# Strassen products summed in the matmul banks and read in between, in the feed-forward layers and the gated unit

## The chip, the cores and the metric

The kernel runs on one core of one Trainium2 chip. The metric is the device time of one execution in microseconds (us); the time of the kernel before is the median of three runs. Engines are named as in the profile: PE (TensorE, with PEld for its weight loads), DVE (VectorE), ACT (ScalarE), POOL (GpSimd), SP (whose queue issues most loads).

## The reference, cut to what matters

A two-layer backbone over 1024 tokens of width 1024, all in fp32. Layer 0 mixes by long convolutions and differential attention, layer 1 by a gated unit over chunks of 128 tokens; each layer ends with a feed-forward net with a short convolution. The change touches what follows the attention of layer 0.

```
x = x + g1 * mix_x                                   # mix: (... ) @ w_out
h = modulate(rmsnorm(x, norm_ffn_g[i]), sh2, sc2)
a = dwconv3(h @ w_up, conv_w, conv_b)                # 1024 -> 2 x 2816, three taps over time
g, u = jnp.split(a, 2, axis=-1)
x = x + g2 * ((silu(g) * u) @ w_down)                # 2816 -> 1024
...
u, v = jnp.split(gelu(h @ w_in + b_in), 2, axis=-1)  # gated unit: 1024 -> 2 x 1024
s = einsum('gts,bnsgc->bntgc', w_s, layernorm(v)) + b_s
mix_x = (u * s) @ w_out
```

## The kernel before

Activations lie transposed, features on the 128 partitions and the 1024 tokens along a row. A product W^T h is made by one step of Strassen's scheme in Winograd's form: W and h are cut into halves both ways, and seven products M1 to M7 of half-sized blocks are taken, not eight. With U2 = M1 + M6 the blocks of the result are C11 = M1 + M2, C12 = U2 + M5 + M3, C21 = U2 + M7 + M4 and C22 = U2 + M7 + M5; C[i, l] holds the features of half i and the tokens of half l. Sums of blocks of W (S1 to S4, `wsums`) and of h (T1 to T4) are made on the way. Every fp32 operand is split into a rounded part and the rest (`hilo`): ACT casts it (L1152), then POOL or DVE subtracts (L128), and `mm3` adds three matmuls hi*hi, hi*lo and lo*hi in one bank. A bank holds 128 x 512 fp32; the pool `pb` has all eight. A "unit" `u` is a tile of 128 x 1024 fp32 in SBUF.

After the attention come: the output projection (`out_proj`), the up phase and down phase of the first feed-forward net, the up phase of the gated unit's half u, its half v, its output projection, and up and down phase of the second net.

An **up phase** (`up_steps`) goes pair by pair: two tiles of 128 output features, one from either half of W's columns, 22 pairs in a net and 4 in the gated unit. In a pair each product is 12 matmuls into one bank. M1 is copied by ACT to both halves of c1 (L1317); the six others are added by DVE where they belong (L1326), M5 in two places, so that DVE has seven additions of 128 x 512 that read a bank. `post` then hands c1 and c2 to generators: in a net four DVE operations of the short convolution (L124, u<-u,cols,u), a scaled copy and a SiLU on ACT (L1520, L1532), a product on DVE, and for each second pair four subtractions on POOL (`spill`), whose results are stored for the down phase. The first three pairs of a phase go product by product (`EARLY`), since M1 and M2 need only the first half of the normed tokens.

A **down phase** (`down_steps`) goes product by product: four banks, 11 tiles k of rows in a net (4 in the gated unit), 12 matmuls for each k, then `accum` adds the four banks to x with the gate (DVE, L124, x<-b,mods,x), M1, M6 and M7 to both halves of a row at once where they belong to two blocks. When both blocks of a half of the tokens are complete, its norm starts beside the next products (`norm`, through `Later`), which also makes the blocks B11 to T4 for the next phase. The gated unit's half v is of this kind, with `accum` of its own.

The program is written out in one order for all engines. `run` issues for each step the preparation of later steps (`prep`, mostly three steps ahead) before the step's own matmuls and evictions, and `Later` inserts the side work; each engine executes its instructions in the order in which they stand. Beside the first net's phases `mods1` computes the modulation vectors of layer 1 (DVE, L124, u<-wraw,siluc,u).

## Time and profile before

| | |
|---|---|
| three runs | 2901.98, 2897.4, 2897.93 us; median 2897.93 |
| profiled execution: span | 2897.8 us, within 0.2 us of the median |
| busy share of the span | PE 85%, PEld 67%, DVE 81%, POOL 56%, ACT 37% |
| first net: up phase, down phase | 1049 to 1557, 1557 to 1811 us |
| gated unit: u, v, output projection | 1811 to 1907, 1907 to 1996, 1996 to 2116 us |
| second net: up phase, down phase and end | 2116 to 2640, 2640 to 2898 us |

The profiled execution's own time is its span; nothing of note lies around it. The phases' borders are where PE begins the first product of each. PE's matmuls are pipelined, so a busy share under 100% in the table of stages is time in which PE had nothing that it could start. The names of tiles leave out their numbers, so `u` stands for every unit and `b` for every bank; what an instruction does is read from its line and its shapes.

### The profile page before, as it was taken

The page shows a single profiled execution, that of the slowest core. Times are in us where ns is not written, and L with a number is a line of the kernel's source. Part 1 is how long each engine was busy: PE and PEld are TensorE (multiplying, and loading weights), DVE is VectorE, ACT ScalarE, POOL GpSimd, SP SyncE. Part 2 cuts the span into 40 slices and gives each one's busy share as a digit, 9 for nine tenths or more (in the row PEclk, how much of TensorE's full clock was granted, in tenths as well). Part 3 has the DMA queues.
Part 4 walks back from the last instruction along what each step waited for, and adds up shares of the span by engine and source line. Part 5 has one row for each costly group of instructions (what it writes and reads, how often), then busy time and mean ns, then how long its engine had stood idle before and what let it go on. Part 6 is the DMA issues. An engine that isn't in the chain of part 4 may idle for free. (4 is left out here: it accounts for less than half of the span.)

```text
span 2897.8 us, 29893 instructions
## 1 busy us (share of the span) xinstructions
PE 2461.0 (85%) x10776; PEld 1949.6 (67%) x10776; DVE 2345.8 (81%) x2467; ACT 1075.4 (37%) x1561; POOL 1624.7 (56%) x986
## 2 busy tenths in 40 slices
PE   6899667777988679999998799899669999999897
PEld 2897556565766457777776687677547777776676
DVE  4666887866998889999998987859988888887944
ACT  2322011015764344433343344532254343344242
POOL 1323565545444755645556787535665655657785
PEclk9899878888999889999999999999889999999999
DMA  7243121256732412434347654153021323227322
GB/s 269 69 143 114 66 87 46 84 183 200 209 122 84 174 65 78 161 122 149 118 145 255 231 164 129 44 186 110 23 79 59 100 85 102 86 85 269 133 91 102
DMA packets 137572, 363.93 MB, mean 126 GB/s; under 512 B 12587, under 2 KB 25391, under 8 KB 135248
## 3 DMA queue, kind: packets, MB, share of 16 engines
q1 hardware_dynamic: 90768, 259.25, 27.8%
q10 hardware_dynamic: 46656, 102.78, 9.4%
q8 instruction: 85, 1.39, 0.2%
q14 instruction: 63, 0.52, 0.1%
HBM read 271.80 MB, written 90.18 MB: 125 GB/s over the span
## 5 line engine op out<-in xcount | busy, mean ns | idle before, releaser
L149 PE MATMUL b<-u,u 128*128 128x512 f32 x5780 | 1422.9, 404 | 199.0 <-POOL u L128 125.7
L149 PEld LDWEIGHTS b<-u,u 128*128 128x128 f32 x5780 | 1104.1, 195 | 504.7 <-POOL u L128 172.0
L128 POOL TENSOR_TENSOR u<-u,u 128x512 fp32r<-128x512 f32 (+2 forms) x641 | 1043.3, 1650 | 602.5 <-ACT u L1152 431.2
L128 DVE TENSOR_TENSOR u<-u,u 128x512 f32<-128x512 f32 (+2 forms) x569 | 641.1, 1156 | 169.9 <-ACT u L1152 91.4
L1152 ACT CAST u<-u 128x512 fp32r<-128x512 f32 x772 | 439.1, 616 | 584.9 <-DVE u L128 400.4
L124 DVE SCALAR_TENSOR_TENSOR u<-u,cols,u 128x1023 f32<-128x1023 f32 x176 | 301.2, 1714 | 11.2 <-ACT u L1520 9.9
L128 DVE TENSOR_TENSOR u<-u,b 128x512 f32<-128x512 f32 (+1 forms) x368 | 248.1, 690 | 19.1 <-PE b L149 12.8
L128 POOL TENSOR_TENSOR f<-f 128x256 f32<-128x256 f32 (+2 forms) x99 | 124.7, 1273 | 211.0 <-DVE f L128 183.1
L149 PE MATMUL b<-x,u 128*128 128x512 f32 x1008 | 242.9, 394 | 0.0
L149 PEld LDWEIGHTS b<-x,u 128*128 128x128 f32 x1008 | 188.6, 187 | 46.0
L128 DVE TENSOR_TENSOR f<-f 128x256 f32<-128x256 f32 (+3 forms) x178 | 178.6, 1052 | 1.1
L124 DVE SCALAR_TENSOR_TENSOR x<-b,mods,x 128x512 f32<-128x512 f32 (+1 forms) x140 | 125.0, 938 | 37.2 <-PE b L149 37.2
L149 PE MATMUL pj<-hh,whi 128*128 128x512 f32 x320 | 130.2, 407 | 24.7 <-DVE t L124 14.0
L1520 ACT ACTIVATE u<-u,cols 128x1024 f32<-128x1024 f32 x88 | 109.2, 1244 | 111.3 <-DVE u L128 97.3
L128 POOL TENSOR_TENSOR p<-p,p 128x1280 f32<-128x1280 f32 x27 | 79.5, 2945 | 97.0 <-ACT p L880 76.5
L149 PE MATMUL pj<-hh,wlo 128*128 128x512 f32 x320 | 127.6, 399 | 3.5 <-DVE wlo L128 1.9
L149 PE MATMUL pj<-hl,whi 128*128 128x512 f32 x320 | 128.9, 403 | 0.0
L1532 ACT ACTIVATE u<-u 128x1024 f32<-128x1024 f32 x44 | 46.7, 1061 | 211.3 <-DVE u L124 211.2
L128 POOL TENSOR_TENSOR wlo<-wraw,whi 128x1024 fp32r<-128x1024 f32 x24 | 63.7, 2655 | 76.9 <-ACT whi L143 73.8
L869 ACT ACTIVATE p<-s,nx 128x1280 f32<-128x1280 f32 x64 | 85.0, 1329 | 43.2 <-DVE nx L865 39.2
L149 PE MATMUL s<-f,f 128*128 128x512 f32 (+1 forms) x288 | 82.3, 416 | 17.5 <-ACT t L768 9.9
L865 DVE TENSOR_REDUCE nx<-s 128x1 f32<-128x1280 f32 x64 | 94.5, 1480 | 2.2 <-PE s L149 1.5
(215 smaller groups left out, 2984.7 us busy)
## 6 DMA issues: line engine op xcount, KB each, us to landing
u<-wup SPq DMA_DIRECT2D x88, 512.0 KB, 3.7
Td<-u ACTq DMA_DIRECT2D x66, 512.0 KB, 3.2
u<-Td SPq DMA_DIRECT2D x56, 512.0 KB, 4.4
wraw<-modw SPq DMA_DIRECT2D x48, 512.0 KB, 3.7
u<-wdown SPq DMA_DIRECT2D x40, 512.0 KB, 7.1
wraw<-modw0b SPq DMA_DIRECT2D x32, 512.0 KB, 4.7
xs<-x ACTq DMA_DIRECT2D x48, 256.0 KB, 2.2
x<-xs SPq DMA_DIRECT2D x24, 512.0 KB, 4.1
```

The lines of the kernel that those rows point to most:

```text
L124: eng.scalar_tensor_tensor(out=o, in0=a, scalar=sc, in1=b, op0=op0, op1=op1)
L128: eng.tensor_tensor(out=o, in0=a, in1=b, op=op)
L149: T.matmul(o, l, r, start=st, stop=sp)
L865: V.reduce_max(out=q.nx, in_=q.s, axis=AX.X, negate=True)
L869: A.activation(q.p[m], q.s, AF.Exp, bias=q.nx, accum_out=q.l[:, m : m + 1])
L1152: A.copy(out=t[:, H0], in_=x)
L1520: A.activation(a, c, AF.Identity, bias=col(f"fb{l}", f), scale=col(f"fw{l}1", f))
L1532: A.activation(g, g, AF.Silu)
```

## The change

In the up phases of both nets and of the gated unit, and in the down phases of both nets and the gated unit's half v, M6 is added by PE onto the bank of M1, M7 onto that of M6, and M3 onto that of M5 (`ONTO`). Between two products that share a bank the bank is read: after M1 (for C11), after M6 (U2, for C12), after M7 (U2 + M7, for C21 and C22), after M5 and after M3. So the second product's first matmul waits for that read. The order of the products changes (`UP_ORDER`, `DOWN_ORDER`) so that at least one other product lies between two on one bank. In an up phase ACT now copies M1, M5, M6 and M4 (128 x 512 each), and DVE adds M2, M3 and, in one instruction of 128 x 1024, M7; `post` follows M7. In a down phase `accum` adds seven results, M7 alone to both blocks (`WHERE2`). The half v adds its bias with the first result that reaches a half row, so the eight separate additions on POOL (`bias`) go. Since C12 and C22 are now complete before C21, the half of the tokens that is normed first is the second one before the gated unit (`LEAD`), with one product beside which it can run; the norm makes T1 first. The two output projections keep the old sums; the gated unit's takes M1 and M2 one after the other, without its special order for the last k. Matmuls, operand splits, `wsums`, convolution and loads stay as many as they were.

```diff
-N0 = ((1, 1), (6, 1), (1, 1), (1, 0))
+N0 = ((1, 1), (1, 6), (1, 1), (1, 0))
...
-DL, DP = (1, 5, 4, 4, 5), ((3, 3, 3, 3, 3, 5, 8),) + ((3,) * 7,) * 4
+DL, DP = (1, 5, 4, 4, 5), ((3, 3, 3, 3, 3, 5, 8),) + ((3,) * 7,) * 2 + ((2,) + (3,) * 6, (3,) * 7)
...
-    def mm(o, l, r, st, sp):
-        T.matmul(o, l, r, start=st, stop=sp)
-
-    def mm3(o, lh, ll, rh, rl, st=True, sp=True):
-        mm(o, lh, rh, st, False)
-        mm(o, lh, rl, False, False)
-        mm(o, ll, rh, False, sp)
+    def mm(o, l, r, st, sp, onto=False):
+
+        T.matmul(o, l, r, start=st and not onto, stop=sp, skip_group_check=onto)
+
+    def mm3(o, lh, ll, rh, rl, st=True, sp=True, onto=False):
+        mm(o, lh, rh, st, False, onto)
+        mm(o, lh, rl, False, False, onto)
+        mm(o, ll, rh, False, sp, onto)
...
-        R, c, x = box[0], HALF[l], list(x)
-        if l == 0:
+        R, c, x, s = box[0], HALF[l], list(x), sqs.s
+        lead = l == LEAD[s]
+        h0, h1 = HALF[LEAD[s]], HALF[1 - LEAD[s]]
+        if lead:
             Stream.T = {n: [None] * 4 for n in BLOCKS}
-        s = sqs.s
...
-            if l == 0:
-                block("B11", k, x[k][:, H0], E(E_11[s], k))
-                block("B21", k, x[k + 4][:, H0], E(E_21[s], k))
+            if lead:
+                block("B11", k, x[k][:, h0], E(E_11[s], k))
+                block("B21", k, x[k + 4][:, h0], E(E_21[s], k))
                 yield 1
-        if l == 0:
+        if lead:
             return
...
-            sub(e, t3[k], z[:, H1], y[:, H1])
-            sub(e, y[:, H1], y[:, H1], y[:, H0])               # T1
-            sub(e, y[:, H0], z[:, H1], y[:, H1])               # T2
-            block("T2", k, y[:, H0], E(E_2[s], k))
+            sub(e, t3[k], z[:, h1], y[:, h1])
+            sub(e, y[:, h1], y[:, h1], y[:, h0])
+            block("T1", k, y[:, h1], E(E_2[s], k))
+            sub(e, y[:, h0], z[:, h1], y[:, h1])
             yield k % 2
         for k in range(4):
-            block("T3", k, t3[k], E(E_3[s], k))
+            block("T2", k, x[k][:, h0], E(E_3[s], k))
             yield k % 2
         for k in range(4):
             y, z = x[k], x[k + 4]
-            sub(E(E_T[s], k), z[:, H0], z[:, H0], y[:, H0])     # T4
-            block("T4", k, z[:, H0], E(E_4[s], k))
+            sub(E(E_T[s], k), z[:, h0], z[:, h0], y[:, h0])
+            block("T4", k, z[:, h0], E(E_4[s], k))
             yield k % 2
-        for n, i in (("T1", 0), ("B22", 4)):
+        for n, i in (("B22", 0), ("T3", 4)):
             for k in range(4):
...
-                T[n][k] = hilo(x[i + k][:, H1], E(E_5[s], i + k), unit if i + k == 0 else xunit)
...
+                T[n][k] = hilo(x[4 + k][:, h1] if i == 0 else t3[k], E(E_5[s], i + k), xunit)
                 yield k % 2
...
+    ONTO = {"M6": "M1", "M7": "M6", "M3": "M5"}
+    UP_ORDER = ("M1", "M2", "M5", "M6", "M4", "M3", "M7")
+    DOWN_ORDER = ("M1", "M2", "M6", "M5", "M7", "M3", "M4")
+    WHERE2 = {"M1": [(0, 0)], "M2": [(0, 0)], "M6": [(0, 1)], "M5": [(1, 1)], "M7": [(1,)], "M3": [(0, 1)],
+              "M4": [(1, 0)]}
...
+    LEAD = (0, 1, 0, 0)
...
-            if m == "M6":
+            if m == "M5":
                 w1, w2 = st_.pop("w1"), st_.pop("w2")
                 s2 = wsums(w1[:, H0], w2[:, H0], w1[:, H1], w2[:, H1], E_U[s])
                 q.update({"M4": w2[:, H1], "M7": w1[:, H0], "M6": s2, "M5": w2[:, H0], "M3": w1[:, H1]})
...
-            ps = bank()
+            ps = st_[m, "ps"] = st_.pop((ONTO[m], "ps")) if m in ONTO else bank()
             wh, wl = st_.pop(m)
             for k in range(4):
                 kk = slice(k * P, (k + 1) * P)
-                mm3(ps, wh[:, kk], wl[:, kk], *Stream.T[BOF[m]][k], k == 0, k == 3)
+                mm3(ps, wh[:, kk], wl[:, kk], *Stream.T[BOF[m]][k], k == 0, k == 3, m in ONTO)
+            h0, h1 = HALF[LEAD[s]], HALF[1 - LEAD[s]]
             if m == "M1":
-                c1 = st_["c1"] = unit()
-                A.copy(out=c1.rearrange("p (a n) -> p a n", a=2), in_=ps[:, None, :].to_broadcast([P, 2, 512]))
-                return
-            c1 = st_["c1"]
-            if m == "M7":
+                st_["c1"] = unit()
+                A.copy(out=st_["c1"][:, h0], in_=ps)
+            elif m == "M2":
+                c = st_["c1"][:, h0]
+                add(V, c, c, ps)
+            elif m == "M5":
                 st_["c2"] = unit()
-            c2 = st_.get("c2")
-            for o, x in {"M2": [(c1, H0)], "M6": [(c1, H1)], "M4": [(c2, H0)], "M5": [(c2, H1), (c1, H1)],
-                         "M3": [(c1, H1)], "M7": [(c2, H1)]}[m]:
-                src = {"M7": c1, "M4": c2}.get(m, o)[:, x if m != "M4" else H1]
-                add(V, o[:, x], src, ps)
-            if m == "M3":
-                post(c1, c2)
-
-        return {m: Step(lambda m=m: use(m), lambda m=m: prep(m), (lambda m=m: load(m)) if m in ("M1", "M6") else None, UL[s],
-                        UP[s][ORDER.index(m)])
-                for m in ORDER}
+                A.copy(out=st_["c2"][:, h1], in_=ps)
+            elif m == "M6":
+                A.copy(out=st_["c1"][:, h1], in_=ps)
+            elif m == "M4":
+                A.copy(out=st_["c2"][:, h0], in_=ps)
+            elif m == "M3":
+                c = st_["c1"][:, h1]
+                add(V, c, c, ps)
+            else:
+                c = st_["c2"].rearrange("p (a n) -> p a n", a=2)
+                add(V, c, c, ps[:, None, :].to_broadcast([P, 2, 512]))
+                post(st_["c1"], st_["c2"])
...
+        return {m: Step(lambda m=m: use(m), lambda m=m: prep(m), (lambda m=m: load(m)) if m in ("M1", "M5") else None, UL[s],
+                        UP[s][UP_ORDER.index(m)])
+                for m in UP_ORDER}
...
-        out = [u[m] for m in ORDER for u in ss[: EARLY[s]]]
+        out = [u[m] for m in UP_ORDER for u in ss[: EARLY[s]]]
         for u in ss[EARLY[s] :]:
-            out += [u[m] for m in ORDER]
+            out += [u[m] for m in UP_ORDER]
...
+            onto = products is DOWN_ORDER and m in ONTO
             if k == 0:
-                banks[m] = [bank() for _ in range(4)]
+                banks[m] = banks.pop(ONTO[m]) if onto else [bank() for _ in range(4)]
             ps = banks[m]
...
         order = [(m, k) for m in products for k in range(nk)]
-        if products is ORDER and nk <= NK and not resident:        # the last k may come late
-            order = [(m, k) for m in ("M1", "M2") for k in range(nk - 1)] + [("M1", nk - 1), ("M2", nk - 1)] \
-                + order[2 * nk :]
         return [Step(lambda m=m, k=k: use(m, k), lambda m=m, k=k: prep(m, k), lambda m=m, k=k: load(m, k), DL[s],
-                     DP[s][ORDER.index(m)])
+                     DP[s][DOWN_ORDER.index(m)])
...
+        last = {"M2": (0, 0), "M4": (1, 0), "M5": (1, 1), "M3": (0, 1)} if where is WHERE else \
+            {"M2": (0, 0), "M7": (1, 1), "M3": (0, 1), "M4": (1, 0)}
...
+        accum = gated_sum(x, gate, where)
...
         def accum(m, j, p):
-            if m == "M1":
-                for t in (j, j + 4):
...
+            for i, l, first in {"M1": [(0, 0, 1)], "M2": [(0, 0, 0)], "M6": [(0, 1, 1)], "M5": [(1, 1, 1)],
+                                "M7": [(1, 0, 1), (1, 1, 0)], "M3": [(0, 1, 0)], "M4": [(1, 0, 0)]}[m]:
+                t = j + 4 * (l if LEAD[1] == 0 else 1 - l)
+                if v[t] is None:
                     v[t] = unit()
-                    A.copy(out=v[t].rearrange("p (a n) -> p a n", a=2), in_=p[:, None, :].to_broadcast([P, 2, 512]))
-                return
-            for i, l in {"M2": [(0, 0)], "M6": [(None, 1), (1, 0)], "M7": [(1, 0), (1, 1)], "M4": [(1, 0)],
-                         "M5": [(None, 1)], "M3": [(0, 1)]}[m]:
-                y = v[j + 4 * l]
-                if i is None:
-                    y, p_ = y.rearrange("p (a n) -> p a n", a=2), p[:, None, :].to_broadcast([P, 2, 512])
-                else:
-                    y, p_ = y[:, HALF[i]], p
-                add(V, y, y, p_)
-
-        def bias():
-            for t in range(NK):
-                add(E(E_B[0], t), v[t], v[t], k_["bv"])
-                yield 1
+                y = v[t][:, HALF[i]]
+                add(V, y, k_["bv"][:, HALF[i]] if first else y, p)
...
-                yield 1 - l
-            yield MIXWAIT
+                yield (1 - l) * (t % 2)
+            if l:
+                yield MIXWAIT
...
         def done(m):
-            if m == "M1":
-                Later.add(bias(), BW)
-            elif m == "M6":
+            if m == "M6":
                 Later.add(offsets())
                 Later.add(loads_u(), LW)
+            elif m == "M3":
+                Later.add(center(0))
             elif m == "M4":
-                Later.add(center(0))
-            elif m == "M3":
                 Later.add(center(1))
...
+        steps += down_steps(3, 4, ap["wso"], lambda m, k: None, bprep, acc, dn, (x, x_src), products=ORDER)
```

What stands on DVE in one pair of the second net's up phase, in the middle of the phase. Before (b_16089 is M6, b_16108 M7, b_16127 M4, b_16144 M5, b_16169 M3; the four rows of 128x512 without a b are `wsums`, the row of 128x1024 the gated product):

```order
L128 TENSOR_TENSOR u_16059<-u_16059,b_16089 128x512
L128 TENSOR_TENSOR u_16083<-u_16083,u_16040 128x1024
L128 TENSOR_TENSOR u_16121<-u_16059,b_16108 128x512
L128 TENSOR_TENSOR u_16014<-u_16014,u_16064 128x512
L128 TENSOR_TENSOR u_16161<-u_16064,u_16014 128x512
L128 TENSOR_TENSOR u_16064<-u_16064 128x512
L128 TENSOR_TENSOR u_16014<-u_16014,u_16161 128x512
L128 TENSOR_TENSOR u_16121<-u_16121,b_16127 128x512
L128 TENSOR_TENSOR u_16121<-u_16121,b_16144 128x512
L128 TENSOR_TENSOR u_16059<-u_16059,b_16144 128x512
L124 SCALAR_TENSOR_TENSOR u_16183<-u_16121,cols,u_16183 128x1023
L128 TENSOR_TENSOR u_16059<-u_16059,b_16169 128x512
```

After (b_15861 is M2, b_15881 M5 and then M3, b_15838 M1, M6 and M7 in turn):

```order
L128 TENSOR_TENSOR u_15851<-u_15851,b_15861 128x512
L124 SCALAR_TENSOR_TENSOR u_15875<-u_15706,cols,u_15875 128x1023 x2
L128 TENSOR_TENSOR u_15807<-u_15807,u_15856 128x512
L128 TENSOR_TENSOR u_15950<-u_15856,u_15807 128x512
L128 TENSOR_TENSOR u_15856<-u_15856 128x512
L128 TENSOR_TENSOR u_15875<-u_15875,u_15832 128x1024
L128 TENSOR_TENSOR u_15807<-u_15807,u_15950 128x512
L128 TENSOR_TENSOR u_15851<-u_15851,b_15881 128x512
L128 TENSOR_TENSOR u_15894<-u_15894,b_15838 128x1024
L124 SCALAR_TENSOR_TENSOR u_15971<-u_15894,cols,u_15971 128x1023 x2
```

Seven additions from banks have become three. The four sums of weights now stand behind the convolution of the pair before and ahead of the additions of M3 and M7, and the convolution's first operation on c2 (u_15894) stands right behind M7's addition, with ACT's scaled copy between the two.

What stands on ACT at the same places. Before (b_16046 is M1; L1317 copies it, L1520 is the convolution's scaled copy, L1532 the SiLU, L1152 a cast, DMA a store's issue):

```order
L1152 CAST u_16021<-u_16016 128x512
L1420 DMA Td_5969<-u_15991 128x2x512
L1520 ACTIVATE u_16040<-u_15970,cols 128x1024
L1152 CAST u_16043<-u_15867 128x512
L1317 COPY u_16059<-b_16046 128x1024
L1152 CAST u_16066<-u_15913 128x512
L1520 ACTIVATE u_16083<-u_15910,cols 128x1024
L1152 CAST u_16086<-u_15913 128x512
L1152 CAST u_16105<-u_15867 128x512
L1532 ACTIVATE u_16083<-u_16083 128x1024
L1413 DMA Td_5969<-u_16083 128x512
```

After (L1330 copies M1, L1336 M5, L1338 M6, L1340 M4; L1541 is the scaled copy, L1553 the SiLU, L1153 a cast):

```order
L1541 ACTIVATE u_15875<-u_15706,cols 128x1024
L1153 CAST u_15878<-u_15664 128x512
L1336 COPY u_15894<-b_15881 128x512
L1153 CAST u_15898<-u_15664 128x512
L1153 CAST u_15915<-u_15807 128x512
L1153 CAST u_15932<-u_15807 128x512
L1553 ACTIVATE u_15875<-u_15875 128x1024
L1338 COPY u_15851<-b_15838 128x512
L1153 CAST u_15955<-u_15856 128x512
L1430 DMA Td_5969<-u_15875 128x512
L1340 COPY u_15894<-b_15918 128x512
L1541 ACTIVATE u_15971<-u_15894,cols 128x1024
```

Three more copies from banks stand between casts and the pieces of the convolution: M6's stands behind the SiLU of the pair before, and two casts of the next pair have moved ahead of that SiLU and of the store.

## Rows read from the trace of the kernel before

**Rows 1.** Page, part 1: busy us, share of span, instructions by engine.

```profile
PE 2461.0 (85%) x10776; PEld 1949.6 (67%) x10776; DVE 2345.8 (81%) x2467; ACT 1075.4 (37%) x1561; POOL 1624.7 (56%) x986
```

**Rows 2.** Windows by stage: length, busy us (instructions) by engine, granted clock.

```profile
core 0: us, PE busy (x) PEld busy (x) DVE busy (x) ACT busy (x) POOL busy (x), PEclk, DMA share, GB/s
1049.00:1557.00 508.00, 462.15 (x1923) 365.47 (x1922) 482.11 (x471) 203.18 (x280) 270.94 (x160) 0.95 0.38 126
1557.00:1811.00 254.00, 226.61 (x982) 180.78 (x983) 210.93 (x193) 109.82 (x192) 193.90 (x120) 0.97 0.58 193
1907.00:1996.00 89.00, 83.48 (x364) 66.20 (x364) 70.45 (x92) 27.30 (x40) 46.21 (x28) 0.98 0.37 125
1996.00:2116.00 120.00, 89.41 (x390) 69.68 (x389) 106.52 (x122) 34.59 (x60) 75.32 (x55) 0.89 0.20 71
2116.00:2640.00 524.00, 468.61 (x1921) 364.66 (x1919) 445.91 (x435) 216.81 (x304) 313.03 (x196) 0.97 0.27 88
2640.00:2898.00 258.00, 226.31 (x949) 179.90 (x947) 160.89 (x159) 96.22 (x171) 192.23 (x132) 0.95 0.42 147
```

**Rows 3.** Timeline of PE, first down phase: start, us, operation, count.

```profile
1687.53 52.67 PE L149 MATMUL b<-u,u 128*128 128x512 f32 x231
```

**Rows 4.** Windows: steady pairs of both up phases, the first net's first.

```profile
1183.00:1542.00 359.00, 329.78 (x1406) 262.40 (x1405) 343.94 (x322) 134.42 (x180) 192.35 (x112) 0.97 0.41 135
2255.00:2626.00 371.00, 344.54 (x1435) 269.06 (x1433) 312.84 (x289) 139.28 (x187) 219.36 (x138) 0.99 0.28 91
```

**Rows 5.** DVE's groups, first steady stretch: count | busy, mean ns | idle before.

```profile
L128 DVE TENSOR_TENSOR u<-u,b 128x512 f32<-128x512 f32 x111 | 74.1, 678 | 1.4
```

**Rows 6.** DVE's waits, first steady stretch: us in total, times, longest.

```profile
DVE u L128 <- ACT u L1532: 5.2, 9, 0.6
```

**Rows 7.** DVE's waits, second steady stretch.

```profile
DVE u L128 <- POOL u L128: 37.8, 17, 3.3
DVE u L128 <- ACT u L1532: 10.0, 17, 0.6
DVE u L124 <- ACT u L1520: 6.9, 9, 0.8
```

**Rows 8.** Timeline of DVE in two pairs of the second net.

```profile
2424.53 0.68 DVE L128 TENSOR_TENSOR u<-u 128x512 f32<-128x512 f32 x1
...
2443.45 3.46 DVE L128 TENSOR_TENSOR u<-u,u 128x512 f32<-128x512 f32 x2 [2.48 <-POOL u L128]
2446.84 1.78 DVE L128 TENSOR_TENSOR u<-u 128x512 f32<-128x512 f32 x1
2450.23 2.06 DVE L128 TENSOR_TENSOR u<-u,b 128x512 f32<-128x512 f32 x3
```

**Rows 9.** Timeline of POOL in the second of these pairs.

```profile
2440.91 1.29 POOL L128 TENSOR_TENSOR u<-u 128x512 f32<-128x512 f32 x1
2442.15 7.60 POOL L128 TENSOR_TENSOR u<-u,u 128x512 fp32r<-128x512 f32 x5
```

**Rows 10.** DVE's groups after 1250 us that read banks, by form.

```profile
L124 DVE SCALAR_TENSOR_TENSOR x<-b,mods,x 128x1024 f32<-128x1024 f32 x48 | 59.5, 1273 | 4.5 <-PE b L149 4.5
L124 DVE SCALAR_TENSOR_TENSOR x<-b,mods,x 128x512 f32<-128x512 f32 x72 | 50.6, 740 | 32.7 <-PE b L149 32.7
...
L128 DVE TENSOR_TENSOR u<-u,b 128x1024 f32<-128x1024 f32 x8 | 9.5, 1213 | 0.0
```

**Rows 11.** POOL's groups, gated unit's u and v.

```profile
L128 POOL TENSOR_TENSOR u<-u,u 128x1024 f32<-128x1024 f32 x8 | 21.0, 2636 | 19.3 <-PE b L149 16.8 <-DVE u L128 2.5
```

**Rows 12.** Timeline of ACT in the pair of rows 9.

```profile
2447.00 0.62 ACT L1152 CAST u<-u 128x512 fp32r<-128x512 f32 x1 [5.84 <-DVE u L128]
...
2450.93 1.25 ACT L1520 ACTIVATE u<-u,cols 128x1024 f32<-128x1024 f32 x1 [3.31 <-DVE u L128]
...
2452.59 1.00 ACT L1317 COPY u<-b 128x1024 f32<-128x1024 f32 x1
```

**Rows 13.** Timeline of PE in the pair of rows 9.

```profile
2443.47 5.75 PE L149 MATMUL b<-u,u 128*128 128x512 f32 x24 [1.07 <-POOL u L128]
```

23 lines of the change are left out of this document (11 added, 12 removed).

## The prediction

> **What bounds the kernel now.** I read the page's busy shares first: no engine is full over the whole span, PE comes nearest with 85% [rows 1]. So the stages come next [rows 2]. The change touches those from 1049 us on: up and down phase of the first net (508 and 254 us), the gated unit, up and down phase of the second net (524 and 258 us). Undisturbed, PE needs 52.67/231 = 0.228 us for a matmul [rows 3]; a pair of an up phase is 84 matmuls, so 19.15 us is PE's floor for it.
>
> Steady pairs, without the first ones of a phase, show two different limits [rows 4]. In the first net 16 pairs take 359 us, 22.4 us each, and DVE is busy for 343.9 of them: 21.5 us a pair, idle 0.94. DVE is the bound there, 3.3 us above PE's floor. In the second net, where `mods1` has gone, 17 pairs take 371 us, 21.8 us each, but DVE works only 312.8/17 = 18.4 us of a pair. Its idle 3.4 us are a chain of in-order queues: the waits name POOL with 37.8/17 = 2.2 us a pair, the SiLU with 0.59, the scaled copy with 0.41 [rows 7]. In the first net the SiLU costs 5.2/16 = 0.33 us a pair [rows 6]. Neither net runs at PE's pace, so less work on DVE can show in the time.
>
> **The change, part by part.** An addition of 128 x 512 from a bank takes 0.678 us [rows 5]. Of M7's new addition, 128 x 1024 from one bank, the nearest row is the 1.213 us of the half v's wide additions [rows 10]. A pair's seven additions, 4.75 us, become 2 x 0.678 + 1.213 = 2.57 us: DVE loses 2.18 us. ACT's copy of 1.00 us [rows 12] becomes four of half the width, between 1.0 us in all (half time each plus nothing) and 4.0 us (no shorter at all): 0 to 3 us more a pair, on an engine that is busy 134.4 of 359 us [rows 4]. As work that is hidden; as position it is not free (below).
>
> How much of 2.18 us is real depends on POOL. In the second net's trace a one-operand DVE operation of 128 x 512 takes 0.68 us in one pair and 1.78 us in another, where POOL is in a string of 7.60/5 = 1.52 us operations that take 1.29 us alone; the additions from a bank, right behind, take 2.06/3 = 0.69 us each, as always [rows 8, 9]. So additions from banks run beside POOL for nothing, and operations whose inputs are all in SBUF do not. If what is removed were only time in which POOL could work, the operations left would meet POOL more often. POOL is busy 192.35/359 = 54% and 219.36/371 = 59% of the time [rows 4]; if that share of the gain is lost, 2.18 x 0.46 = 1.0 and 2.18 x 0.41 = 0.89 us a pair are left. The Trainium skill, "SBUF — State Buffer", section "Who interferes with whom", says that a DVE instruction with two SBUF inputs and a GpSimd instruction that reads SBUF lock each other out, while a DVE instruction with one SBUF input does not contend. By that rule all that is removed is of the kind that does not contend, which speaks against the change; the sum by it would be the one of rival C, and the rows above agree on the kinds.
>
> The new order also moves waits. ACT's scaled copy, 1.25 us [rows 12], now stands between M7's addition and the convolution's first DVE operation, with nothing for DVE in between: up to 1.25 us a pair in the first net, where no such wait is in the rows, and 1.25 - 0.41 = 0.84 in the second. The SiLU's wait goes the other way: the sums of weights now stand between the convolution and the product that waits for the SiLU, so 0.33 and 0.59 us can vanish. The casts of the next pair's operands, which stood behind the store and the SiLU, stand ahead of them, which should feed POOL earlier and so shorten the 2.2 us of POOL waits in the second net.
>
> *First net, per pair.* Best: -2.18 - 0.33 = -2.5. Worst: -1.0 + 1.25 - 0.33 = -0.1, say 0. I take -1.1, just under the middle, since the new wait's place is certain from the order. 22 - 3 = 19 pairs: -21 us (0 to -48).
>
> *Second net, per pair.* Best: PE's floor, 21.8 - 19.15 = -2.67. Worst: -0.89 + 0.84 - 0.59 = -0.6. I take -1.8, just past the middle, since the POOL waits are the larger part of what DVE idles. 19 pairs: -34 us (-12 to -51).
>
> *First pairs* of the three phases (nine) and the gated unit's fourth: DVE loses 10 x 2.18 = 22 us, but there PE also waits for norms and loads; -8 (0 to -22).
>
> *Down phases of the nets.* M1 goes from eight operations of 1.273 to four of 0.740 us (-7.2), M6 from four of each to four short ones (-5.1), M5 from eight short ones to four (-3.0) [rows 10]: -15.3 us of DVE in each. But PE is busy 226.6 of 254 and 226.3 of 258 us there, DVE 210.9 and 160.9 [rows 2], and these bursts lie beside the next product, whose four banks are other banks. -4 for both (0 to -16).
>
> *Half v.* DVE: 8 x 1.213 + 24 x 0.678 = 26.0 us become 32 x 0.678 = 21.7; POOL's eight bias additions of 2.636 us go [rows 11]. Against that, the layer norm of the half that is ready first begins behind the sixth and not the fifth product (48 x 0.228 = 10.9 us later), and the unit's output projection, with DVE busy 106.5 of 120 us beside it [rows 2], loses the order in which M2 covered M1's last rows (three steps of 12 matmuls, 8.2 us). Both delays in full would be 19 us, the saved DVE work hides 4: I take +4 (-4 to +19).
>
> *From first net to gated unit.* The half that is normed first has one product (132 x 0.228 = 30 us) and not two beside it. The norm's chain has to fit in there; 0 (-4 to +10).
>
> Matmuls, splits and loads are as many as before: nothing. Sum: -21 - 34 - 8 - 4 + 4 + 0 = -63. The profiled span is 2897.8 us and the median 2897.93, so no correction is needed: 2835 us.
>
> **Rivals.** B, full relief: POOL does not get in the way and ACT's new wait hides behind the sums of weights. -48 - 51 - 22 = -121: 2778 us. For it speaks that DVE idles for others in the second net; against it, that PE's floor is met nowhere in rows 4.
>
> C, POOL takes it back: the additions that go cost POOL nothing, the rest of DVE meets POOL more densely, and the scaled copy's wait comes on top: the worst ends of both nets, 0 and -12, and nothing else: 2886 us. For it speak the 0.68 and 1.78 us of rows 8; against it, that it takes both a full loss to POOL and the scaled copy's whole wait in every pair.
>
> D, slower: the bank's hand-off. A product that goes onto another's bank waits for the read in between. Before, ACT's copy of M1 began at 2452.59 [rows 12], while M1's last matmuls are, by the program's order, the first ten of the 24 that began at 2443.47 [rows 13], so they ended about 2443.47 + 10 x 0.24 = 2445.9: 6.7 us late, behind casts that themselves waited for DVE. No one cared, since M2 had its own bank. Now M6 waits for the copy of M1 with two products between, 24 x 0.228 = 5.5 us (one between M5 and M3, and M7 waits for M6's copy, which stands behind a SiLU). Two such lags a pair cost about 2 x (6.7 - 5.5) = 2.4 us at most, 2 us as a fair figure; 48 pairs x 2.0 = 96, against the sum's 63 of gains: +33, 2931 us. It decides from 63/48 = 1.3 us a pair. Against it: the casts that stood ahead of M1's copy and waited now stand elsewhere, and PE's matmuls stand in the same queue three steps behind their preparation.
>
> E, no change: gains and the hand-off's stalls cancel, 2892 to 2904 us.
>
> **How the numbers follow.** My forecast, 2808 to 2862 us (either net's term off by half): 0.50. B, 2762 to 2808: 0.17. C, 2862 to 2892: 0.18. E: 0.07. D: 0.08. What this kernel's measurement can tell from no change is about 0.2%, 5.8 us. Faster by more: 0.50 + 0.17 + 0.18 = 0.85; within: 0.07; slower: 0.08. The range leaves out D, E, and the outer rims of B and C (0.02 each): 2780 to 2888 us.
>
> **What the profile after would show.** Right, if: additions from banks of 128 x 512 fall from seven to two a pair at 0.68 us, and one of 128 x 1024 near 1.21 us appears; the up phases last 508 - 21 and 524 - 34 us, less some early gain; DVE's waits show the scaled copy with about 1 us a pair and POOL well under 2.2 us in the second net. C, if DVE operations from SBUF alone grow in mean duration by what the additions gave up. B, if steady pairs come at 19 to 20 us. D, if PE's waits name ACT's copies (or DVE's additions of M3, M7) for over 1 us a pair. The gated unit is wrongly sized if 1907 to 2116, 209 us before, moves by more than 10 us. The prediction falls if ACT's queue becomes the chain: each copy from a bank then stands behind a cast or a piece of convolution that waits for DVE, and DVE for PE.

## The result and the profile after

The changed kernel takes 2923.46 us (median of four runs, 2921.09 to 2928.11), the kernel before 2897.66 beside it: a ratio of 1.0083, 95% interval 1.0068 to 1.0098. It is slower by 24 us by the ratio (26 between the medians), where 63 us less were forecast. The profiled execution's span is 2922.1 us. Page, part 1:

```profile
PE 2470.3 (85%) x10776; PEld 1959.1 (67%) x10776; DVE 2234.8 (76%) x2251; ACT 1116.6 (38%) x1697; POOL 1605.0 (55%) x978
```

Against [rows 1] DVE has lost 111 us and 216 instructions, PE does the same number of matmuls. The windows by stage (columns as in [rows 2]; first net up, down, gated unit u, v, output projection, second net up, down and end):

```profile
1051.00:1571.00 520.00, 464.38 (x1924) 363.90 (x1923) 438.76 (x387) 227.04 (x348) 268.53 (x163) 0.95 0.37 122
1571.00:1835.00 264.00, 228.15 (x983) 185.23 (x982) 184.88 (x167) 105.66 (x183) 185.65 (x113) 0.94 0.55 187
1835.00:1947.00 112.00, 89.16 (x345) 69.55 (x344) 71.85 (x85) 53.69 (x88) 50.48 (x33) 0.86 0.23 80
1947.00:2031.00 84.00, 83.47 (x378) 67.78 (x377) 56.54 (x93) 21.29 (x34) 24.52 (x20) 1.00 0.47 157
2031.00:2148.00 117.00, 86.34 (x377) 67.57 (x376) 110.63 (x121) 34.66 (x60) 78.33 (x56) 0.87 0.17 59
2148.00:2664.00 516.00, 467.94 (x1923) 364.22 (x1922) 419.10 (x350) 238.42 (x371) 322.97 (x197) 0.97 0.27 90
2664.00:2922.00 258.00, 225.74 (x948) 180.01 (x947) 155.51 (x144) 96.23 (x169) 188.66 (x131) 0.95 0.42 145
```

DVE works less in every stage but the output projection, and three stages are longer all the same: the first net's up phase by 12, its down phase by 10, the gated unit's u by 16 us (nearly 5 of them because the same 345 matmuls keep PE busy for 89.16 us at a mean granted clock of 0.86, where it was 84.48 at 0.93). The row of u before, for comparison:

```profile
1811.00:1907.00 96.00, 84.48 (x345) 65.90 (x344) 72.67 (x92) 48.30 (x73) 44.94 (x30) 0.93 0.27 98
```

Since PE's matmuls are the same in number and, nearly, in stage, one can ask in two traces when the n-th of them begins. The lag behind the kernel before, worked out so, in us (*e3_mods_earlier*, *e8_lead_first* and *e11_prep_deeper* are experiments described below; where a stage orders its matmuls in another way, a lag can be off by 2 to 3 us):

```
at (us in the kernel before)         after  e3_mods_earlier  e8_lead_first  e11_prep_deeper
1049  first net, up phase              1.6       -1.3             1.3            -4.2
1183  its early pairs are through     11.0       10.1            12.7             7.7
1542  16 pairs later                   8.3        4.2             6.8           -12.3
1557  down phase                      13.5       11.1            13.7            -6.9
1811  gated unit, u                   24.0        2.6            12.5             5.0
1907  v                               40.1       16.5            18.8            19.6
1996  output projection               32.3        8.6             9.5            11.7
2116  second net, up phase            32.4        8.7            10.3            11.8
2255  its early pairs are through     40.2       16.2            15.6            14.2
2626  17 pairs later                  23.6       -0.5            -0.9           -18.3
```

Ahead of the first row nothing that matters differs: matmuls there lie up to 5 us apart from run to run, which is noise of one execution. The steady pairs gave 2.7 us in the first net and 16.6 in the second; v and the output projection gave 7.7. What is lost lies at the borders: 9.4 us in the first net's early pairs, 7.8 in the second's, and 31.8 between the first net's last pair and v.

### The profile page after: what moved, and what is told of

It is laid out like the page before. It is cut to its first block, busy times and chain, and to the rows that moved or that the text cites. A ratio compares the mean times of both kernels' runs of the same rounds, so it can differ in the third digit from the quotient of the medians.

```text
span 2922.1 us, 29654 instructions
## 1 busy us (share of the span) xinstructions
PE 2470.3 (85%) x10776; PEld 1959.1 (67%) x10776; DVE 2234.8 (76%) x2251; ACT 1116.6 (38%) x1697; POOL 1605.0 (55%) x978
## 5 line engine op out<-in xcount | busy, mean ns | idle before, releaser
L150 PE MATMUL b<-u,u 128*128 128x512 f32 (+1 forms) x5624 | 1381.8, 404 | 183.8 <-POOL u L128 100.7
L150 PEld LDWEIGHTS b<-u,u 128*128 128x128 f32 x5624 | 1078.8, 196 | 474.0 <-POOL u L128 138.0
L128 POOL TENSOR_TENSOR u<-u,u 128x512 fp32r<-128x512 f32 (+1 forms) x631 | 1024.7, 1646 | 589.9 <-ACT u L1153 435.5
L128 DVE TENSOR_TENSOR u<-u,u 128x512 f32<-128x512 f32 (+2 forms) x559 | 664.2, 1218 | 216.2 <-ACT u L1153 123.8
L1153 ACT CAST u<-u 128x512 fp32r<-128x512 f32 x760 | 436.0, 617 | 425.3 <-DVE u L128 265.0
L150 PE MATMUL b<-x,u 128*128 128x512 f32 x1152 | 279.5, 396 | 13.9 <-ACT u L1338 13.9
L150 PEld LDWEIGHTS b<-x,u 128*128 128x128 f32 x1152 | 214.3, 187 | 71.5 <-ACT u L1338 20.7
L1541 ACT ACTIVATE u<-u,cols 128x1024 f32<-128x1024 f32 x88 | 109.3, 1243 | 222.4 <-DVE u L128 202.4
L128 DVE TENSOR_TENSOR u<-u,b 128x512 f32<-128x512 f32 (+1 forms) x176 | 141.9, 823 | 59.0 <-PE b L150 58.9
L124 DVE SCALAR_TENSOR_TENSOR x<-b,mods,x 128x512 f32<-128x512 f32 (+1 forms) x116 | 95.6, 868 | 33.7 <-PE b L150 33.7
L1553 ACT ACTIVATE u<-u 128x1024 f32<-128x1024 f32 x44 | 46.7, 1061 | 172.0 <-DVE u L124 167.3
```

The lines of the kernel that those rows point to most:

```text
L124: eng.scalar_tensor_tensor(out=o, in0=a, scalar=sc, in1=b, op0=op0, op1=op1)
L128: eng.tensor_tensor(out=o, in0=a, in1=b, op=op)
L150: T.matmul(o, l, r, start=st and not onto, stop=sp, skip_group_check=onto)
L1153: A.copy(out=t[:, H0], in_=x)
L1541: A.activation(a, c, AF.Identity, bias=col(f"fb{l}", f), scale=col(f"fw{l}1", f))
L1553: A.activation(g, g, AF.Silu)
```

## The experiments

Sixteen kernels ran in four groups, each beside the kernel before on the same chip. Ratios are to the kernel before with their 95% intervals.

**The borders.** The largest single wait is in the down phase. Timeline of PE in the changed kernel, behind M7's last row of matmuls:

```profile
1737.76 10.13 PE L150 MATMUL b<-u,u 128*128 128x512 f32 x44
1761.86 3.57 PE L150 MATMUL b<-ones,u 128*128 128x1 f32 x16 [13.97 <-DVE x L124]
1765.30 5.05 PE L150 MATMUL b<-u,u 128*128 128x512 f32 x13
```

What waits is the small matmul with which `mods1` reduces one of its vectors. From the start of M5 until M7 is read, the changed order holds all eight banks (four for M1, M6, M7, four for M5, M3), so its bank is one that DVE must first empty, and DVE gets to that behind splits of later operands. Timeline of DVE there:

```profile
1760.54 2.46 DVE L124 SCALAR_TENSOR_TENSOR x<-b,mods,x 128x1024 f32<-128x1024 f32 x2
```

*e3_mods_earlier* moves that reduction to where four banks are free:

```diff
-MD, MY = 45, 3
+MD, MY = 42, 3
```

> The changed kernel with the first number of MD, MY = 45, 3 set to 42: mods1 begins three steps earlier, so the small matmul that reduces its fifth vector finds a free bank in M6 of the first net's down phase and no longer has to stand behind M7's last rows, where all eight banks are held. Theory 'borders, by banks': the one wait of PE of 14.0 us there goes, -10 to -14 us. If the norm behind it is what is late anyway, the 14 us show up again before the gated unit: 0 to -4 us.

Measured: 2902.60 us, 1.0011 (0.9997 to 1.0024), 21 us less. In its trace the lag over that place stays at 5.3 us, while it jumps from 12.5 to 28.4 in the changed kernel: 16 us, the 14.0 and the reduction itself, which takes 3.57 us behind the wait and 1.95 in this run (PE had stood, and the granted clock is 0.54 from 1760 to 1770 us, near the lower of its two levels, 1.2 and 2.4 GHz; here it stays at 1.00). From the down phase's start to v the lag grows by 5.4 us in this run and by 26.6 in the changed kernel: the 21 us of the time, more than the 10 to 14 expected. So nothing of it comes back later.

*e2_down0_old* takes the first net's down phase back, and with it the half of the tokens that is normed first (its layer norm of one half of v then reads tiles to which M4 isn't added yet):

```diff
-    LEAD = (0, 1, 0, 0)
+    LEAD = (0, 0, 0, 0)
...
+                            products=ORDER if l == 0 else DOWN_ORDER)
```

> The changed kernel with the first net's down phase as before (old order of products, old sums by DVE, first half of the tokens normed first, two products beside the norm). Theory 'borders': from the last third of this phase to the gated unit's third early product the changed kernel loses some 30 us (the lag behind the kernel before grows from 10.6 to 40.1 us), which come back: -22 to -32 us. Theory 'hand-off': the loss is in the up phases' pairs, and DVE gets its 15 us of additions back in this phase: 0 to +8 us.

Measured: 2892.32 us, 0.9973 (0.9962 to 0.9984), 31 us less: theory 'borders'. From 1557 to 1907 its lag grows by 2.9 us. It is 10 us below e3_mods_earlier, but 7 of them lie in v and the output projection (lag falling by 15.0 there, by 7.8 in e3_mods_earlier), where its layer norm starts on tiles that aren't complete; they can't be credited to the down phase. *e8_lead_first* keeps the sums over M1, M6 and M7 in the banks and changes the order, so that the first half is complete early:

```diff
+    LEAD_ORDER = ("M1", "M2", "M6", "M4", "M7", "M5", "M3")
+    WHERE3 = {**WHERE2, "M5": [(1, 1), (0, 1)]}
...
+            onto = m in ONTO and (products is DOWN_ORDER or products is LEAD_ORDER and m != "M3")
```

> The changed kernel with another order in the first net's down phase and the half v: M1, M2, M6, M4, M7, M5, M3, with M3 in banks of its own (DVE adds M5 to two blocks). The first half of the tokens is complete behind M7 again, with two products beside its norm, and only M1, M6, M7 share banks; mods1 begins three steps earlier, as in the run before. Theory 'borders': the 18 us of PE's wait for a bank and 6 to 10 of the 12 us at the border to the gated unit come back, against 6 more short additions a phase: 2923 - 18 - 6 = about 2898, 2890 to 2903. If the border's loss came from something else (the new copies on ACT): no lower than the 2902.6 of the run with mods1 earlier alone.

Measured: 2898.71 us, 0.9991 (0.9981 to 1.0), as expected and 25 us below the changed kernel. But it holds e3_mods_earlier's edit too, which gave 21 of these alone: the two intervals overlap, and between 1557 and 1907 the lag grows by 5.1 us here and by 5.4 there. What the new order wins at the unit's start (6.3 us lost from 1811 to 1907, 13.9 in e3_mods_earlier) it gives up in the down phase before (1.2 us won there, against 8.5). That it saves time on the whole isn't shown. With one product beside the norm, PE waits for it in the changed kernel (timeline of PE at the unit's start):

```profile
1846.73 1.86 PE L150 MATMUL b<-ones,u 128*128 128x1 f32 x8 [6.83 <-DVE u L128]
...
1870.65 5.03 PE L150 MATMUL b<-u,u 128*128 128x512 f32 x12 [4.05 <-POOL u L128]
...
1889.17 1.22 PE L150 MATMUL b<-u,u 128*128 128x512 f32 x2 [3.86 <-ACT u L1153]
```

All three stand in e3_mods_earlier as well (6.83, 4.05 and 3.84 us). In e8_lead_first the first has fallen to 1.27 us; the two others, waits of early products for their blocks, stand in it unchanged. *e7_early_m6* asks whether they hang on which block comes first:

```diff
-        out = [u[m] for m in UP_ORDER for u in ss[: EARLY[s]]]
+        out = [u[m] for m in ("M1", "M2", "M6", "M5", "M4", "M3", "M7") for u in ss[: EARLY[s]]]
```

> The changed kernel with M6 ahead of M5 in the first three pairs of an up phase, and the norm making T2 ahead of T1 (as the kernel before did). PE waits 6.3 us for T2 at the first early M6 of the first net and again in the gated unit. If the early pairs lose because of which block comes first: -6 to -18 us over the three phases. If T1 is then as late as T2 was, or ACT's new copies between the casts are what holds them up: -3 to +3 us.

Measured: 2920.57 us, 1.0066 (1.0046 to 1.0085): 3 us less, near noise. The first net's early pairs lost as much as ever (9.2 us). Why they lose 9 us stays open; two further runs give a hint, no more: with a split a pair moved from POOL to DVE (e10_splits_dve, below) the two nets' early pairs lose 4.7 and 3.4 us, with earlier preparation (e11_prep_deeper) 11.9 and 2.4.

**The steady pairs.** DVE's groups that read a bank in the changed kernel's steady stretches, first net and second (columns as in [rows 5]; the row of 1744 ns reads no bank, it is the second net's split on DVE, to which the section on the rivals comes back):

```profile
L128 DVE TENSOR_TENSOR u<-u,b 128x512 f32<-128x512 f32 x32 | 21.6, 675 | 0.5 <-PE b L150 0.5
L128 DVE TENSOR_TENSOR u<-u,b 128x1024 f32<-128x1024 f32 x15 | 18.1, 1209 | 1.9 <-PE b L150 1.9
...
L128 DVE TENSOR_TENSOR u<-u,u 128x512 fp32r<-128x512 f32 x17 | 29.7, 1744 | 0.0
L128 DVE TENSOR_TENSOR u<-u,b 128x512 f32<-128x512 f32 x34 | 22.9, 675 | 0.0
L128 DVE TENSOR_TENSOR u<-u,b 128x1024 f32<-128x1024 f32 x17 | 20.5, 1207 | 0.0
```

Two short additions and a wide one a pair, at the durations of the forecast. The windows of these stretches, against [rows 4]:

```profile
1194.00:1550.00 356.00, 327.28 (x1405) 258.49 (x1404) 307.89 (x257) 151.35 (x228) 184.56 (x112) 0.99 0.41 135
2295.00:2649.00 354.00, 337.76 (x1433) 265.36 (x1432) 290.34 (x220) 154.31 (x235) 227.69 (x138) 1.00 0.30 97
```

DVE's busy time fell by 36 us in the first net and 22 in the second, the stretches by 3 and 17. It waits instead (waits of DVE, first net and second):

```profile
DVE u L128 <- POOL u L128: 21.6, 9, 2.4
DVE u L124 <- ACT u L1541: 19.7, 15, 2.9
...
DVE u L128 <- POOL u L128: 35.0, 10, 4.4
DVE u L124 <- ACT u L1541: 21.5, 16, 1.8
```

and PE waits for POOL's splits and, new, for the copies of M1 (L1330) and M6 (L1338) (waits of PE, first net and second):

```profile
PE b L150 <- POOL u L128: 14.3, 15, 1.6
PE b L150 <- ACT u L1330: 9.5, 7, 2.1
PE b L150 <- ACT u L1338: 4.9, 3, 1.9
...
PE b L150 <- POOL u L128: 6.3, 9, 0.7
PE b L150 <- ACT u L1338: 5.8, 8, 0.7
PE b L150 <- ACT u L1330: 3.7, 8, 0.5
```

Eleven runs take these waits apart. The length of the same pairs' matmuls in each trace, in us:

```
                        first net, 16 pairs   second net, 17 pairs
kernel before                  359.0                371.0
  e9_before_extra              365.3                373.3
  e13_before_deeper            357.2                345.6
  e17_before_splits            362.4                379.2
changed kernel                 356.4                354.3
  e1_own_banks                 353.4                352.5
  e5_extra_adds                361.8                357.8
  e6_sums_later                352.3                352.1
  e10_splits_dve               343.7                344.0
  e11_prep_deeper              339.1                338.4
  e12_all                      345.0                350.9
  e14_all_deeper               338.2                337.2
  e15_deeper_splits            341.0                339.7
```

Each number is of one execution. How far chance moves them is seen in four runs that keep the changed kernel's steady pairs and differ elsewhere (e2_down0_old, e3_mods_earlier, e7_early_m6, e8_lead_first; in two of them `mods1` runs three steps earlier beside the first net): 353.2 to 360.3 us in the first net, 354.2 to 354.6 in the second. So some 4 us in the first net say nothing by themselves, while 1 us in the second does.

*e1_own_banks* removes the hand-off of banks:

```diff
-            ps = st_[m, "ps"] = st_.pop((ONTO[m], "ps")) if m in ONTO else bank()
+            ps = bank()
```

> The changed kernel, but in the up phases every product gets a bank of its own, so that no product waits for the read of another's; the sums over banks (M6 on M1, M7 on M6, M3 on M5) are left out there, DVE and ACT do the same instructions as in the changed kernel. Theory 'hand-off' (rival D of the prediction): PE's waits for ACT's copies of M1 and M6, 16 us in the first net's steady pairs and 10 in the second's, are added to the time, so this run is 20 to 35 us below the changed kernel's 2922. Theory 'borders' (the loss lies where one stage meets the next): steady pairs are paced by DVE, POOL and ACT together, the same wait only changes its name, 0 to -10 us.

Measured: 2913.71 us, 1.0054 (1.0035 to 1.0073): theory 'borders'. The copies are gone from PE's waits, and POOL's splits and ACT's casts have taken their place (waits of PE, first net and second):

```profile
PE b L150 <- POOL u L128: 20.8, 15, 2.8
PE b L150 <- ACT u L1153: 8.4, 6, 1.7
...
PE b L150 <- POOL u L128: 16.6, 17, 1.2
```

That is 29.2 and 16.6 us, where the changed kernel's rows add up to 28.7 and 15.8: the wait has changed its name. The pairs are 3.0 and 1.8 us shorter, under a quarter of what the waits for the copies name; the 3.0 is within chance. 4 of the total's 10 us lie ahead of the first pair. The hand-off costs little.

*e5_extra_adds* gives DVE back work of the kind that was taken:

```diff
+            if m in ("M6", "M4"):
+                z = sp.tile([P, 512], F32, tag="sq", name=nm("sq"), bufs=4)
+                add(V, z, st_["c1"][:, h0], ps)
```

> The changed kernel with two more DVE additions of 128 x 512 from a bank in every pair of the up phases (of M6 and of M4, into a scratch tile that nobody reads): 2 x 0.68 = 1.36 us of the kind that the change removed, 48 pairs. If DVE's work still sets the pace of the pairs, +40 to +65 us on 2923. If DVE now has slack and the pace is set by the queues' order (it idles 3.0 us a pair in the first net and 3.8 in the second), +0 to +15 us; then the 2.18 us that the change took off DVE could not come back in the time either.

Measured: 2933.60 us, 1.0109 (1.0092 to 1.0126): +10 us for 65 us of work. DVE, which idles 48 and 64 us in the two nets' pairs, has slack in the changed kernel: its busy time rises by 12.2 and 9.9 us, the pairs get 5.4 and 3.5 us longer. *e9_before_extra* is the same edit on the kernel before.

> The kernel before with the same two further DVE additions of 128 x 512 a pair (of M6 and M4, into a scratch tile), 48 pairs, 65 us of DVE work in all. The prediction took DVE for the bound of the first net's pairs. If it was, the first net's 22 pairs alone give +30 us and the total is +40 to +65 us on the kernel before. If DVE had slack there too, and a chain through the queues set the pace, +5 to +20 us, like the +10 us that they cost in the changed kernel.

Measured: 2920.52 us, 1.0062 (1.0044 to 1.0081): +20 us, the edge of the second range. The pairs show 6.3 and 2.3 us for 21.8 and 23.1 us of additions. That looks like slack on DVE, but the additions did not go into its idle time. The first net's window in e9_before_extra, and two of DVE's groups there, in the kernel before and in e9_before_extra:

```profile
1191.00:1557.00 366.00, 331.74 (x1409) 263.90 (x1409) 349.38 (x356) 135.61 (x182) 191.39 (x114) 0.97 0.41 132
...
L128 DVE TENSOR_TENSOR u<-u,u 128x512 f32<-128x512 f32 x48 | 56.1, 1169 | 6.5 <-POOL u L128 5.9
L128 DVE TENSOR_TENSOR u<-u,u 128x512 fp32r<-128x512 f32 x32 | 33.2, 1036 | 1.0 <-ACT u L1152 1.0
...
L128 DVE TENSOR_TENSOR u<-u,u 128x512 f32<-128x512 f32 x48 | 48.1, 1002 | 14.0 <-POOL u L128 13.8
L128 DVE TENSOR_TENSOR u<-u,u 128x512 fp32r<-128x512 f32 x32 | 29.6, 925 | 0.4 <-ACT u L1152 0.4
```

In the first net DVE's busy time rose by 5.4 us and not by 21.8, because its other operations got shorter, and it idles as before (16.6 us, 15.1 before). The time rose by about what the busy time did. A bound DVE would look like that too, so this run alone doesn't decide whether DVE holds the first net's pairs; e13_before_deeper, below, does more.

*e4_conv_later* and *e6_sums_later* go after DVE's wait for the scaled copy.

```diff
             A.activation(a, c, AF.Identity, bias=col(f"fb{l}", f), scale=col(f"fw{l}1", f))
+            if f >= NF:
+                yield 1
```

> The changed kernel with one step between ACT's scaled copy of c2 and the convolution's first operation on it (the step between the two halves of the convolution goes instead), so that DVE no longer idles right behind M7's addition. If DVE's queue sets the pace of the steady pairs, its waits for the scaled copy, 18.1 us in the first net and 22.8 in the second, come back: -25 to -40 us. If the pace is set by the hand-off of banks or by POOL, 0 to -10 us.

Measured: 2924.04 us, 1.0084 (1.0064 to 1.0105). It says nothing: DVE's order came out the same there, with the copy's wait as long as before. The second edit moves work in between:

```diff
-UL, UP = (9, 8, 8), ((3,) * 7,) * 3
+UL, UP = (9, 8, 8), ((3, 3, 2, 3, 3, 3, 3), (3,) * 7, (3, 3, 2, 3, 3, 3, 3))
```

> The changed kernel with the preparation of M5 (which holds the sums of weights) two steps ahead and not three, in the nets. In the order two of the four sums then stand between M7's addition and the convolution's first operation, so that DVE has work while ACT makes the scaled copy (the earlier run with the convolution a step later had left that order unchanged). If that wait, 18.1 us in the first net's steady pairs and 22.8 in the second's, is on the path: -20 to -40 us. If the path runs through POOL's splits: -8 to +8 us, and the wait goes over into DVE's waits for POOL.

Measured: 2919.60 us, 1.0058 (1.0043 to 1.0073): -4 us in all, -4.1 and -2.2 in the pairs. The wait for the scaled copy is halved (9.4 and 11.2 us, where it was 19.7 and 21.5), and of these 20.6 us at most 6.3 show. That wait isn't the limit either. What is left is POOL and what feeds it.

*e10_splits_dve* and *e17_before_splits* move a split a pair to DVE, in the changed kernel and in the kernel before:

```diff
-E_W, E_D, E_O = ("VGGVGGG", "VGGVGGG", "GGGVGGG"), ("GVGV", "VVGV", "GVGV", "GVGV", "GVGV"), ("GGVV", "GGVG")
+E_W, E_D, E_O = ("VGGVGVG", "VGGVGGG", "GGGVGVG"), ("GVGV", "VVGV", "GVGV", "GVGV", "GVGV"), ("GGVV", "GGVG")
```

> The changed kernel with M6's split of the weights on DVE and not on POOL, in both nets: 44 operations of some 1.6 us leave POOL, and come to DVE at 0.68 to 1.78 us. If POOL's splits are the slow part of the chain, the steady pairs get shorter: -10 to -30 us in all, about 0.3 to 0.6 us a pair. If the chain is DVE's own queue with ACT's pieces in it (scaled copy, SiLU), the new work lies on it: +5 to +40 us.

Measured: 2893.23 us, 0.9982 (0.9965 to 0.9999), 30 us less. Its windows:

```profile
1191.00:1534.00 343.00, 322.88 (x1404) 258.58 (x1403) 297.97 (x273) 151.14 (x228) 164.07 (x96) 0.99 0.43 140
2273.50:2617.50 344.00, 335.83 (x1435) 266.25 (x1433) 265.21 (x238) 154.35 (x237) 202.29 (x121) 1.00 0.31 101
```

DVE has 33 splits more here, and its busy time is 10 and 25 us lower than in the changed kernel: a split on DVE takes 0.77 and 0.68 us on average, where it took 1.23 and 1.74.

> The kernel before with M6's split of the weights on DVE and not on POOL in both nets, the same edit that gave the changed kernel 30 us. DVE is busy 96% of the first net's steady pairs there, so 16 x 0.68 to 1.78 us more must show: 0 to +25 us, if the change's slack on DVE is what the edit uses. If POOL was the slow part there too: -15 to -30 us.

Measured: 2908.59 us, 1.0037 (1.0018 to 1.0055), 11 us more. The same edit wins on one kernel and loses on the other; that DVE is fuller in the kernel before (347.2 of 362 us in this run's first net) fits, but no run shows that this is why.

*e11_prep_deeper* and *e13_before_deeper* prepare operands a step earlier and load them a step earlier:

```diff
-UL, UP = (9, 8, 8), ((3,) * 7,) * 3
+UL, UP = (10, 8, 10), ((4,) * 7, (3,) * 7, (4,) * 7)
```

> The changed kernel with the operands of the nets' up phases prepared four steps ahead and not three (and loaded one step earlier). If the pace of the steady pairs is the latency of the chain cast, split, product within the preparation's reach, more reach shortens them: -10 to -30 us. If the chain is closed over a whole pair (M7's addition, scaled copy, convolution, SiLU, product, sums of weights, splits), the reach changes nothing there: -5 to +10 us, since the units that are held longer can also make other work wait.

Measured: 2878.67 us, 0.9914 (0.9881 to 0.9947), 45 us less. Windows and, for the first net, the waits of PE and of DVE in it:

```profile
1191.00:1530.00 339.00, 323.99 (x1406) 262.43 (x1405) 296.31 (x258) 151.68 (x228) 195.85 (x113) 0.98 0.43 143
2269.00:2608.00 339.00, 331.17 (x1437) 268.62 (x1436) 267.07 (x223) 157.00 (x241) 232.06 (x138) 1.00 0.31 101
```

```profile
PE b L150 <- ACT u L1330: 10.2, 6, 2.7
PE b L150 <- ACT u L1338: 4.5, 4, 1.8
```

```profile
DVE u L124 <- ACT u L1541: 38.2, 16, 6.7
...
DVE u L128 <- POOL u L128: 2.3, 1, 2.3
```

PE's 14.3 us of waits for POOL are gone, and DVE's fell from 21.6 to 2.3. PE's waits for M1's and M6's copies stay (14.7 us). The earlier loads are not what helps: in the changed kernel's steady pairs neither PE, DVE nor ACT waits for a load.

> The kernel before with the operands of the nets' up phases prepared four steps ahead and loaded one step earlier, the same edit that gave the changed kernel 45 us. If the reach of the preparation hid the change's gain and DVE holds the kernel before just behind it, the kernel before gains little, 0 to -15 us. If the reach set the pace of both alike, it gains as much, -35 to -50 us.

Measured: 2883.74 us, 0.9939 (0.9918 to 0.9961), 14 us less: none in the first net (359.0 to 357.2), 25.4 in the second. Its windows:

```profile
1184.00:1541.00 357.00, 332.03 (x1406) 266.04 (x1405) 319.60 (x319) 133.02 (x178) 191.69 (x111) 0.96 0.40 136
2259.00:2604.00 345.00, 334.19 (x1432) 266.69 (x1431) 272.33 (x288) 136.86 (x184) 233.06 (x137) 1.00 0.27 94
```

DVE idles 37 us in the first and the time is not shorter, so at four steps it isn't DVE's work that holds the kernel before there. What does isn't settled. The waits of PE in the first net, in the kernel before and in e13_before_deeper, name POOL's splits with nearly the same time:

```profile
PE b L149 <- POOL u L128: 23.2, 13, 4.1
PE b L149 <- DVE u L128: 4.4, 7, 1.1
PE b L149 <- ACT u L1152: 1.5, 3, 0.9
...
PE b L149 <- POOL u L128: 20.5, 13, 3.8
PE b L149 <- ACT u L1152: 4.4, 4, 1.8
```

**Together.** *e12_all* has the edits of e8_lead_first, e7_early_m6 and e6_sums_later; *e14_all_deeper* those of e8_lead_first, e7_early_m6 and e11_prep_deeper; *e15_deeper_splits* adds that of e10_splits_dve.

> The changed kernel with the order of the run with M3 in banks of its own (M1, M2, M6, M4, M7, M5, M3 in the first net's down phase and the half v, mods1 three steps earlier), with M6 ahead of M5 in early pairs, and with the sums of weights prepared a step later. If what the three gave apart adds up (25, 3 and 4 us off 2923): about 2891, 2882 to 2896, which would be faster than the kernel before by 0.1 to 0.6%. If the two small ones were chance: 2898.

Measured: 2880.85 us, 0.992 (0.9891 to 0.995), 43 us below the changed kernel, some 10 more than the sum of the parts. 7 of them stand in the first net's steady pairs (345.0 us, 352.3 in e6_sums_later); why isn't shown.

> The changed kernel with the repaired border (M3 in banks of its own in the first net's down phase and the half v, mods1 earlier), M6 ahead of M5 in early pairs, and preparation four steps ahead. If the 25 us of the border, some 3 of the early pairs and the 45 of the reach add up: 2923 - 73 = 2850, 2840 to 2862.

Measured: 2851.21 us, 0.9831 (0.9802 to 0.9861): as the sum said, and 1.7% faster than the kernel before.

> The run with the repaired border and preparation four steps ahead, and M6's splits on DVE as well. If reach and POOL's load are two limits, each of which holds alone: 10 to 25 us below that run, 2828 to 2842. If both edits loosen the same chain: within 6 us of it. PE's floor leaves 19.15 us a pair, some 2 us a pair less than the changed kernel's.

Measured: 2849.95 us, 0.983 (0.9802 to 0.9859), the same, as if reach and splits loosen one chain. In the second net another reading is open: PE is busy 330 of 337 us there in e14_all_deeper, so little was left to win.

## Why the prediction was wrong

**The step that failed: "DVE is the bound there"**, and with it that less DVE work must show. In the first net DVE's busy time fell by 36 us and the pairs got 2.6 us shorter, which is within chance. The step went by DVE's busy share, 343.9 of 359 us [rows 4], and by DVE's waits; what PE waits for was not read: 23.2 of the 29.2 us that PE idles in these pairs before the change stand beside POOL's splits, 4.4 beside DVE. What held the changed kernel's pairs is how operands reach PE: in order through sums of weights, ACT's casts and POOL's splits, prepared three steps ahead. Taking 2.18 us a pair off DVE left that where it was, and DVE's idle time went from 0.94 to 3 us a pair. One step more of preparation took 17.3 and 15.9 us off the two nets' pairs (e11_prep_deeper), a split a pair moved from POOL 12.7 and 10.3 (e10_splits_dve). What holds the first net's pairs in the kernel before stays open: with four steps DVE idles 37 us there and the pairs are 1.8 us shorter.

At four steps, e11_prep_deeper against e13_before_deeper is 339.1 against 357.2 us in the first net, 1.13 us a pair, where the forecast was 1.1; 338.4 against 345.6 in the second, 0.42 a pair against 1.8. At three steps it was 0.16 and 0.98. That 1.13 meets 1.1 is luck: the forecast reckoned with a bound DVE, and at four steps DVE idles 37 us in the one kernel and 43 in the other.

**Borders: 0 forecast, 26.6 us lost** from the down phase's start to v (the worst end given for that border was +10). The text did not look at the banks at all there: "whose four banks are other banks" was true of the next product, and false of a ninth user, the reduction of `mods1`. With that moved, 5.4 us remain (e3_mods_earlier), inside the forecast's range. The text also said that the norm's chain "has to fit in there", beside one product, and didn't work out whether it does. PE waits 6.83 us for it, but that two products beside it save time on the whole isn't shown (e8_lead_first).

**Early pairs: -8 forecast, +17 measured** in the two nets. The blocks' new order was looked at only for the steady pairs; the cause of the loss stays open.

**Half v and output projection: +4 forecast, -7.7 measured.** v takes 84 us, 89 before, and PE is busy all but 0.5 of them, all but 5.5 before. That DVE's relief (70.45 us of 89 before, 56.54 of 84 after) hid both delays is likely; no run tests it.

**Right:** durations (0.675 and 1.209 us against 0.678 and 1.213), DVE's new wait for the scaled copy (19.7/16 = 1.2 us a pair against "up to 1.25", 21.5/17 = 1.3 in the second net), the SiLU's wait (5.2 to 1.1 us in the first net), and additions from banks that don't slow down beside POOL. One sign failed: DVE's waits for POOL in the second net, 35.0/17 = 2.06 us a pair, are not "well under 2.2", and in the first net they rose from 5.9 to 21.6 us.

**The rivals.** D named the right sign for another reason: without the hand-off the nets' steady pairs are 3.0 and 1.8 us shorter (e1_own_banks), where 96 in all were forecast. C expected almost no gain from the pairs, for a reason that isn't theirs: in the second net the split on DVE went from 0.679 to 1.744 us and one of the four sums back from 1.263 to 0.685, so that 22 of 36 us of relief were left, but DVE's time wasn't what counted. The rule of the Trainium skill, "SBUF — State Buffer", section "Who interferes with whom", holds in kind (additions from a bank took 0.675 us in both nets, whatever POOL did); the "one-operand" operation of 0.68 and 1.78 us in the prediction adds two halves of one tile (the third operation of `wsums`), so it has two inputs in SBUF and is of the kind that contends. The loss that rival C built on the rule is not in the first net's rows, where DVE's busy time fell by as much as the additions (36 us, and 34 by their rows). B's pace, 19 to 20 us a pair, needs the deeper preparation and is met in the second net alone (338.4/17 = 19.9 us, 339.1/16 = 21.2 in the first).

## What to carry to other kernels

An engine that is busy 96% of a stretch is not shown to be its bound: read what the engine that should never stand is waiting for. When a known amount of harmless work is added as a test, look at the busy time before drawing the conclusion: here 21.8 us of additions raised DVE's by 5.4, since its other operations got shorter. Where in-order queues feed each other through a fixed look-ahead, relief on one engine may need a step more of look-ahead, or work moved into the gap, before it shows. When accumulators are shared to save work, count for each moment how many are free for everybody else, small side work above all.
